# Projections' products in another order: the weights' low part last in a tile's first groups and first in its last ones

## Chip, cores and metric

The kernel runs on one core of one Trainium2 chip. The metric is the device time of one execution in microseconds. Engines: TensorE (PE; its weight loads are listed as PEld), VectorE (DVE), ScalarE (ACT), GpSimd (POOL), SyncE (SP, which issues most DMAs).

## What is computed

Two layers of a hybrid diffusion backbone over 256 latent tokens and 256 context tokens, width 1024, batch 1. Cut to what matters:

```python
for l in range(DEPTH):                       # 2 layers
    u  = modulate(layer_norm(h),  sh1, sc1)  # latent tokens
    uc = modulate(layer_norm(hc), csh1, csc1)  # context tokens
    m, mc = mixer(u, uc, w_in[l], ..., w_out[l])
    h = layer_norm_affine(DEEPNORM_ALPHA * h + g1 * m, ...)
    ...
    y = moe(tok, w_router, b_router, w_expert_gate[l], w_expert_up[l], w_expert_down[l])
    h = layer_norm_affine(DEEPNORM_ALPHA * h + g2 * y, ...)
```

Each mixer begins with a projection `u @ w_in` of all 512 tokens (1024 to 3328 columns in layer 0, to 2592 in layer 1) and ends with one, `concat(...) @ w_out` (1024 to 1024). Layer 0's mixer is windowed attention beside a two-way gated scan; layer 1's is a gated linear attention beside a Fourier mix. Behind each mixer stands a layer of 16 experts, of which each token takes two.

## The kernel before, in words

Tokens stand in four blocks of 128: 0 and 1 are context, 2 and 3 latent. Projections are made from parts: each float32 operand is split into a high part (a rounded copy, type `fp32r`, made by an ACT cast, L360 in `split`) and a low part (what the copy left out, made by a DVE subtraction, L362). `mm3` (L374 to L379) sums three of the four products of parts, high x high, high x low and low x high, for each of the 8 slices k of 128 rows: 24 products in one group, into one region of PSUM, k by k with the three interleaved. Index 0 in `PASSES` is a high part, 1 a low part.

Weights come in tiles: `load_w` reads a tile of 128 x 8 x 256 from memory into one of `NW = 3` slots `w`, on SP's queue; `split_w` (L366) makes `wh` (2 buffers) and `wl` (1 buffer) from it. In mixer 1 `cols_w` (L1123) does the same in two halves, also with two `wh` and one `wl`.

- Mixer 0 (`feat` at L704, `toks` at L710): `feat` takes the weights as the first (stationary) operand and gives features by tokens, `toks` takes them as the second (moving) operand and gives tokens by features. A tile of 256 columns has two calls (t = 0, 1), which is two groups of 24 (`feat`, 512 tokens wide) or four (`toks`, two blocks of 256 columns in each call): 96 products. The loop at L819 goes over ten tiles; the last eight are `toks`. Evictions are ACT's or DVE's (`ev_f`, `ev_hi`, `ev_gate`; `qT` at L774 with the rotary step `rope`, L719, behind it).
- Output projections (`out_proj`, L428): four weight tiles `wo` in four buffers each for high and low; a block's two halves of the output take two groups of 24 each.
- Mixer 1: three gate tiles (two groups each, blocks 2 and 3), two q tiles (two groups of 96 rows), then four tiles of keys, values and rank columns (`kvr_w`, L1241, four groups, blocks 0 to 3, 296 columns), and one for the Fourier input (`z_cols`, L1265). While gates and q run, `block` (L1143) steps blocks 0 and 1 through normalisation (`yk`, L1157), transposes by PE (L1164), modulation (ACT L1170 and DVE L1172 into `xT`) and the split into the two parts of `uT`, which the keys and values of these blocks need.

The program writes instructions in Python's order, and a scheduler of the framework then lists them on each engine by its own estimates of what is ready, within data dependencies and buffers. An engine runs its list in order, so an instruction that waits holds up all behind it. Products of a group need not stand together in PE's list.

Of the kernel before, what the change touches and what calls it, by code (L numbers as in the profile page):

```python
# [116 lines left out]
def hybrid_dit_kernel(ctx: ExitStack, tc: tile.TileContext, *aps, dbg=None, stop=99):  # L117
    nc = tc.nc
# [23 lines left out]
    def mmt():  # L142
        return mm.tile([128, 512], FP, name="mm", tag="mm")
# [222 lines left out]
    def split_w(pool, src, k, n, lobufs=1, eng=None):  # L366
        w = load_w(src, k, n)
        wh = pool.tile([128, k, n], FR, name="wh", tag="wh")
        wl = pool.tile([128, k, n], FR, name="wl", tag="wl", bufs=lobufs)
        split(wh, wl, w, eng)  # L370
        return wh, wl

    PASSES = ((0, 0), (0, 1), (1, 0))

    def mm3(ps, lhs, rhs, nk):

        for k in range(nk):
            for n, (i, j) in enumerate(PASSES):
                nc.tensor.matmul(ps, lhs(i, k), rhs(j, k), start=(k == 0 and n == 0), stop=(k == nk - 1 and n == 2))  # L379

    def xn_transpose(xT, xn, b):

# [45 lines left out]
    def out_proj(h, b, mixk, wos, g1, p):  # L428

        for n in range(2):  # L430
            ps = mmt()
            for q in range(2):
                mm3(ps[:, q * 256:(q + 1) * 256], mixk, lambda i, k: wos[n * 2 + q][i][:, k, :], 8)
            tm = p.tile([128, 512], FP, name="opt", tag="opt", bufs=2)
            cs = slice(n * 512, n * 512 + 512)
            nc.vector.tensor_tensor(tm, ps, g1[:, cs], op=OP.mult)
            nc.vector.scalar_tensor_tensor(h[b][:, cs], h[b][:, cs], ALPHA, tm, op0=OP.mult, op1=OP.add)
# [203 lines left out]
    def mixer0(s0, sr):  # L641
# [10 lines left out]
        qT = mC.tile([128, 4, 512], FP, name="qT")  # L652
# [4 lines left out]
        hqT, hi = hx[:, 0:4], hx[:, 4:8]  # L657
# [15 lines left out]
        with ExitStack() as sa:  # L673
            m1 = pool(sa, "m1")
            up = [m1.tile([128, 8, 512], FR, name=f"uT{i}") for i in range(2)]
# [17 lines left out]
            wt = split_w(m2, win[:, 512:768], 8, 256)  # L693
# [7 lines left out]
                return None  # L701
            row_bcast(snk, attn_sink[0:1, :])

            def feat(wt, o, dst_fn):  # L704

                ps = mmt()
                mm3(ps, lambda i, k: wt[i][:, k, o:o + 128], lambda i, k: up[i][:, k, :], 8)
                dst_fn(ps)

            def toks(wt, n, o, dst_fn, bp):  # L710

                ps = mmt()
                for i2 in range(2):
                    b = bp * 2 + i2
                    mm3(ps[:, i2 * n:(i2 + 1) * n], lambda i, k: up[i][:, k, b * 128:(b + 1) * 128],
                        lambda i, k: wt[i][:, k, o:o + n], 8)
                dst_fn(ps[:, 0:2 * n].rearrange("p (b n) -> p b n", b=2), bp)

            def rope(t):  # L719
                ps = trt()  # L720
                nc.tensor.matmul(ps[:, 0:256], C("perm"), t, start=True, stop=True)
                r = mq.tile([128, 256], FP, name="rot", tag="rot")
                nc.vector.tensor_tensor(r, ps[:, 0:256], C("sin"), op=OP.mult)
                nc.vector.tensor_tensor(t, t, C("cos"), op=OP.mult)
                nc.vector.tensor_tensor(t, t, r, op=OP.add)
# [45 lines left out]
            for j in range(2):  # L771
                wt = split_w(m2, win[:, j * 256:(j + 1) * 256], 8, 256)
                for t in range(2):
                    feat(wt, t * 128, lambda ps: nc.scalar.mul(qT[:, 2 * j + t, :], ps, 0.125))  # L774
                    rope(qT[:, 2 * j + t, 256:512])
            nc.vector.tensor_copy(mk[:, 0, :], C("band0"))
            nc.vector.tensor_copy(mk[:, 1, :], C("band1"))
# [41 lines left out]
            for off, ev in ((1792, None), (768, lambda i: ev_f(0, i)), (1280, lambda i: ev_f(1, i)), (2304, ev_hi),  # L819
                            (2816, ev_gate)):  # L820
                for i in range(2):
                    wt = split_w(m2, win[:, off + i * 256:off + (i + 1) * 256], 8, 256)
                    for t in range(2):
                        if ev:
                            toks(wt, 256, 0, ev(i), t)
                        else:
                            feat(wt, t * 128, lambda ps: nc.scalar.copy(hqT[:, 2 * i + t, :], ps))
                            for g_ in lws:
                                next(g_, None)

# [209 lines left out]
        wos = []  # L1040
        src = w_out_even[0]
        for n in range(4):
            w = wp.tile([128, 8, 256], FP, name="w", tag="w")
# [63 lines left out]
    def mixer1(s0, sr, h, rh, hc, y_d, pw, g2s, pre, yks, ring):  # L1107
# [6 lines left out]
        qT = m0.tile([96, 4, 256], FP, name="qT1")  # L1114

        kvr = m0.tile([128, 4, 1184], FP, name="kvr")
# [3 lines left out]
        up = [m0.tile([128, 8, 512], FR, name=f"uT1{i}") for i in range(2)]  # L1120
        mw = pool(sm, "nw", 2)

        def cols_w(o, n, ws=None):  # L1123

            wh = mw.tile([128, 8, 296], FR, name="wh", tag="wh")[:, :, 0:n]
            wl = mw.tile([128, 8, 296], FR, name="wl", tag="wl", bufs=1)[:, :, 0:n]
            for q in range(2):
                w = ws[q] if ws else load_w(win[q * 512:(q + 1) * 512, o:o + n], 4, n)
                split(wh[:, q * 4:q * 4 + 4, :], wl[:, q * 4:q * 4 + 4, :], w)
            return wh, wl  # L1130

        def toks(wt, n, b, dst_fn):

            ps = mmt()
            mm3(ps[:, 0:n], lambda i, k: up[i][:, k, b * 128:(b + 1) * 128], lambda i, k: wt[i][:, k, :], 8)
            dst_fn(ps[:, 0:n], b)

        with ExitStack() as sa:
# [52 lines left out]
            start = len(nc.cur_bb.bb.instructions)  # L1191
# [4 lines left out]
            wt = cols_w(1568, 256, pre)  # L1196
# [7 lines left out]
            for oo in (0, 256, 512):  # L1204
                wt = cols_w(1568 + oo, 256) if oo else wt
                for b in (2, 3):
                    def ev(ps, b, oo=oo):
                        o = gate[:, b - 2, oo:oo + 256]
                        nc.scalar.activation(o, ps, AF.Silu)
                        nc.vector.tensor_tensor(o, o, gnb[:, oo:oo + 256], op=OP.mult)  # L1210
                    toks(wt, 256, b, ev)
                    next(ctx_, None)
            for j in range(2):
                wt = cols_w(j * 192, 192)
                for i in range(2):
                    ps = mmt()
                    mm3(ps[0:96, 0:256], lambda p, k: wt[p][:, k, i * 96:(i + 1) * 96],
                        lambda p, k: up[p][:, k, 256:512], 8)
                    nc.scalar.mul(qT[:, 2 * j + i, :], ps[0:96, 0:256], float(96 ** -0.5))
                    next(ctx_, None)  # L1220
            for _ in ctx_:
# [19 lines left out]
        def kvr_w(i):  # L1241
            o = 296 * i
            wt = cols_w(384 + o, 296)
            for b in range(4):
                toks(wt, 296, b, lambda ps, b: (nc.scalar.copy if b % 2 else nc.vector.tensor_copy)(
                    kvr[:, b, o:o + 296], ps))
                yield

        def decays():
# [166 lines left out]
        wos = []  # L1416
        for n in range(4):
            w = load_w(w_out_odd[0][:, n * 256:(n + 1) * 256], 8, 256)
# [601 lines left out]
```

## Time and profile before

| | |
|---|---|
| median of 3 runs | 1478.98 us (1477.32 to 1482.2) |
| the profiled execution | 1483.32 us |
| its span, first to last instruction | 1481.1 us |
| mean granted TensorE clock | 0.923 |
| instructions | 18934 |

The profile is one execution; its span is what the views below divide. Times in them are microseconds from the span's start, unless a column says ns. "Granted clock" is the share of full speed that the throttle allowed the matmul engine in a stretch. A wait is idle time of an engine, put down to the instruction that ended it; `L379` is a line of the kernel, `mm<-wl,uT` the output and the inputs by the program's names.

### The profile page before, as it was taken

To read this page: it belongs to the slowest core of one execution; us is meant where nothing else is said; L and a number is where in the kernel's file an instruction comes from. 1 tells how busy PE (TensorE), PEld (TensorE's weight loads), DVE (VectorE), ACT (ScalarE), POOL (GpSimd) and SP (SyncE) were. 2 spreads that over 40 slices of the span, in tenths; PEclk is the share of its full clock that TensorE was granted. 3 is DMA by queue.
4 is the path that set the end of the run, shared out by engine and by line. 5 is a ranking of instruction groups with operands and counts; after the bars stand their busy time and mean duration, and the time that the engine had idled before them with its cause. 6 is when DMAs were issued, how large, how long until landed. Compare 5 with 4: busy or idle time off the path is not lost. (4 is left out here: it accounts for less than half of the span.)

```text
span 1481.1 us, 18934 instructions
## 1 busy us (share of the span) xinstructions
PE 1239.4 (84%) x7293; PEld 746.9 (50%) x7293; DVE 609.0 (41%) x1412; ACT 352.3 (24%) x690; POOL 94.8 (6%) x126
## 2 busy tenths in 40 slices
PE   5798888999879569999999964899977788988882
PEld 2678886445559523333333324888537443534330
DVE  4432313665657911211212169636557322223223
ACT  1422212544334111111101033442222210101001
POOL 1000001100111110110100010000010000000000
PEclk9899999999959779999999986999998799999997
DMA  8422123644011599999968953322283799988631
GB/s 274 161 87 86 62 82 99 215 159 127 2 29 72 203 357 368 372 374 340 360 243 317 355 192 101 116 64 90 86 295 127 298 393 395 387 325 312 256 144 59
DMA packets 153255, 310.30 MB, mean 210 GB/s; under 512 B 8629, under 2 KB 40693, under 8 KB 153121
## 3 DMA queue, kind: packets, MB, share of 16 engines
q1 hardware_dynamic: 145456, 293.29, 55.4%
q0 software_dynamic: 6496, 11.74, 2.2%
q10 hardware_dynamic: 1168, 3.49, 0.7%
q8 instruction: 84, 1.38, 0.4%
q14 instruction: 51, 0.41, 0.1%
HBM read 305.86 MB, written 12.06 MB: 215 GB/s over the span
## 5 line engine op out<-in xcount | busy, mean ns | idle before, releaser
L379 PE MATMUL mm<-wh,uT 128*128 128x256 f32 (+2 forms) x960 | 192.6, 297 | 4.1 <-ACT wh L360 3.7
L379 PEld LDWEIGHTS mm<-wh,uT 128*128 128x128 f32 x960 | 159.8, 200 | 10.6 <-ACT wh L360 4.4
L379 PE MATMUL mm<-wl,uT 128*128 128x256 f32 (+2 forms) x480 | 142.6, 298 | 17.0 <-DVE wl L362 17.0
L1511 PE MATMUL mm<-wx,xT 128*64 128x512 f32 x504 | 143.5, 603 | 2.8 <-ACTq L1643 1.2
L379 PEld LDWEIGHTS mm<-wl,uT 128*128 128x128 f32 x480 | 95.7, 199 | 19.9 <-DVE wl L362 19.3
L1511 PEld LDWEIGHTS mm<-wx,xT 128*64 128x64 f32 x504 | 44.9, 138 | 68.7 <-issue 66.4
L362 DVE TENSOR_TENSOR wl<-w,wh 128x2048 fp32r<-128x2048 f32 (+3 forms) x33 | 53.7, 1649 | 60.4 <-PE mm L379 59.8
L1496 DVE TENSOR_TENSOR hs<-hs,mm 64x512 f32<-64x512 f32 x32 | 22.1, 691 | 129.6 <-ACT hs L1495 83.4
L379 PE MATMUL mm<-uT,wh 128*128 128x512 f32 (+1 forms) x208 | 59.3, 374 | 6.1 <-ACT wh L360 6.1
L1511 PE MATMUL ac<-wx,xT 128*64 128x512 f32 x216 | 60.4, 595 | 3.7 <-PEq L1925 2.1
L259 PE MATMUL mm<-w,sT 128*32 128x512 f32 x296 | 52.5, 636 | 11.3 <-DVE rs L307 10.1
L379 PE MATMUL mm<-wo,mx 128*128 128x256 f32 x384 | 51.6, 293 | 6.0 <-ACT wo L360 3.5
L1518 PE MATMUL mm<-wx,hT 128*64 128x512 f32 x192 | 54.9, 597 | 1.7 <-PEq L1658 1.0
L1511 PE MATMUL tr<-wx,xT 128*64 128x512 f32 x200 | 51.8, 617 | 5.1 <-PEq L1925 2.1
L1495 ACT ACTIVATE hs<-mm 64x512 f32<-64x512 f32 x32 | 18.9, 589 | 153.7 <-PE mm L1511 103.2
L360 ACT CAST wh<-w 128x2048 fp32r<-128x2048 f32 (+3 forms) x33 | 45.7, 1387 | 34.4 <-DMA w<-in_w_in_odd_dram 16.6
L379 PEld LDWEIGHTS mm<-wo,mx 128*128 128x128 f32 x384 | 48.7, 198 | 6.8 <-ACT wo L360 3.8
L1511 PE MATMUL ac<-w,xT 128*64 128x512 f32 x104 | 44.6, 617 | 1.5 <-PEq L1925 0.8
L379 PEld LDWEIGHTS mm<-uT,wh 128*128 128x128 f32 (+1 forms) x208 | 36.9, 187 | 13.2 <-ACT wh L360 7.0
L1511 PE MATMUL mm<-w,xT 128*64 128x512 f32 x120 | 43.1, 595 | 0.5 <-PEq L1643 0.5
L1597 DVE COPY ys<-mm 64x512 f32<-64x512 f32 x22 | 15.3, 693 | 67.6 <-ACT ys L1597 64.4
L379 PE MATMUL mm<-uT,wl 128*128 128x512 f32 (+1 forms) x104 | 38.3, 375 | 3.4 <-DVE wl L362 3.4
(486 smaller groups left out, 2113.6 us busy)
## 6 DMA issues: line engine op xcount, KB each, us to landing
wx<-in_w_expert_up_dram SPq DMA_DIRECT2D x45, 1024.0 KB, 9.5
wx<-in_w_expert_gate_dram SPq DMA_DIRECT2D x42, 1024.0 KB, 7.9
wx<-in_w_expert_down_dram SPq DMA_DIRECT2D x42, 1024.0 KB, 8.5
w<-in_w_ada_dram SPq DMA_DIRECT2D x37, 1024.0 KB, 6.2
w<-in_w_expert_down_dram SPq DMA_DIRECT2D x15, 1024.0 KB, 8.7
w<-in_w_in_even_dram SPq DMA_DIRECT2D x13, 1024.0 KB, 5.1
w<-in_w_expert_gate_dram SPq DMA_DIRECT2D x12, 1024.0 KB, 9.7
w<-in_w_expert_up_dram SPq DMA_DIRECT2D x12, 1024.0 KB, 8.0
```

What stands on the lines that cost most here:

```text
L259: nc.tensor.matmul(ps[32 * g:32 * g + 32, :], sT[:, k, :], ws[k // 4][:, k % 4, :], start=k < 4, stop=k >= 4, skip_group_check=True, tile_ ...
L360: nc.scalar.copy(hi, src)
L362: nc.vector.tensor_tensor(lo, src, hi.bitcast(FP), op=OP.subtract)
L379: nc.tensor.matmul(ps, lhs(i, k), rhs(j, k), start=(k == 0 and n == 0), stop=(k == nk - 1 and n == 2))
L1495: nc.scalar.activation(hs, hp[0:64, :], AF.Silu)
L1496: nc.vector.tensor_tensor(hs, hs, hp[64:128, :], op=OP.mult)
L1511: nc.tensor.matmul(hp[i * 64:i * 64 + 64, :], xT(k), ws[2 * i + k // 4][:, k % 4, :], start=k == 0, stop=k == 7, skip_group_check=True, ti ...
L1518: nc.tensor.matmul(yp[n * 64:n * 64 + 64, :], hT[:, k, :], ws[4 + k // 2][:, k % 2, n * 512:(n + 1) * 512], start=k == 0, stop=k == 3, ski ...
L1597: (nc.vector.tensor_copy if n else nc.scalar.copy)(ys[:, ns], yp[rs_, :])
```

## The change

`mm3` no longer interleaves. It makes two lists, the eight products with the weights' low part and the sixteen others, and runs one after the other: the low ones last by default, first with `early`. The argument `w` says which operand is the weights. `early` is set for the later groups of a weight tile: the second call of a tile in mixer 0, blocks 2 and 3 of a `kvr` tile, block 3 of a gate tile, the second q group. The output projections and `z_cols` always have the low ones last. The number of products, their sizes and operands stay.

```diff
@@ -372,11 +372,14 @@
 
     PASSES = ((0, 0), (0, 1), (1, 0))
 
-    def mm3(ps, lhs, rhs, nk):
-
-        for k in range(nk):
-            for n, (i, j) in enumerate(PASSES):
-                nc.tensor.matmul(ps, lhs(i, k), rhs(j, k), start=(k == 0 and n == 0), stop=(k == nk - 1 and n == 2))
+    def mm3(ps, lhs, rhs, nk, w, early=False):
+
+
+        low = [(k, p) for p in PASSES if p[w] for k in range(nk)]
+        high = [(k, p) for k in range(nk) for p in PASSES if not p[w]]
+        order = low + high if early else high + low
+        for n, (k, (i, j)) in enumerate(order):
+            nc.tensor.matmul(ps, lhs(i, k), rhs(j, k), start=n == 0, stop=n == len(order) - 1)
 
     def xn_transpose(xT, xn, b):
 
@@ -430,7 +433,7 @@
         for n in range(2):
             ps = mmt()
             for q in range(2):
-                mm3(ps[:, q * 256:(q + 1) * 256], mixk, lambda i, k: wos[n * 2 + q][i][:, k, :], 8)
+                mm3(ps[:, q * 256:(q + 1) * 256], mixk, lambda i, k: wos[n * 2 + q][i][:, k, :], 8, 1)
             tm = p.tile([128, 512], FP, name="opt", tag="opt", bufs=2)
             cs = slice(n * 512, n * 512 + 512)
             nc.vector.tensor_tensor(tm, ps, g1[:, cs], op=OP.mult)
@@ -701,10 +704,10 @@
                 return None
             row_bcast(snk, attn_sink[0:1, :])
 
-            def feat(wt, o, dst_fn):
+            def feat(wt, o, dst_fn, early=False):
 
                 ps = mmt()
-                mm3(ps, lambda i, k: wt[i][:, k, o:o + 128], lambda i, k: up[i][:, k, :], 8)
+                mm3(ps, lambda i, k: wt[i][:, k, o:o + 128], lambda i, k: up[i][:, k, :], 8, 0, early)
                 dst_fn(ps)
 
             def toks(wt, n, o, dst_fn, bp):
@@ -713,7 +716,7 @@
                 for i2 in range(2):
                     b = bp * 2 + i2
                     mm3(ps[:, i2 * n:(i2 + 1) * n], lambda i, k: up[i][:, k, b * 128:(b + 1) * 128],
-                        lambda i, k: wt[i][:, k, o:o + n], 8)
+                        lambda i, k: wt[i][:, k, o:o + n], 8, 1, bp > 0)
                 dst_fn(ps[:, 0:2 * n].rearrange("p (b n) -> p b n", b=2), bp)
 
             def rope(t):
@@ -771,7 +774,7 @@
             for j in range(2):
                 wt = split_w(m2, win[:, j * 256:(j + 1) * 256], 8, 256)
                 for t in range(2):
-                    feat(wt, t * 128, lambda ps: nc.scalar.mul(qT[:, 2 * j + t, :], ps, 0.125))
+                    feat(wt, t * 128, lambda ps: nc.scalar.mul(qT[:, 2 * j + t, :], ps, 0.125), t > 0)
                     rope(qT[:, 2 * j + t, 256:512])
             nc.vector.tensor_copy(mk[:, 0, :], C("band0"))
             nc.vector.tensor_copy(mk[:, 1, :], C("band1"))
@@ -824,7 +827,7 @@
                         if ev:
                             toks(wt, 256, 0, ev(i), t)
                         else:
-                            feat(wt, t * 128, lambda ps: nc.scalar.copy(hqT[:, 2 * i + t, :], ps))
+                            feat(wt, t * 128, lambda ps: nc.scalar.copy(hqT[:, 2 * i + t, :], ps), t > 0)
                             for g_ in lws:
                                 next(g_, None)
 
@@ -1129,10 +1132,11 @@
                 split(wh[:, q * 4:q * 4 + 4, :], wl[:, q * 4:q * 4 + 4, :], w)
             return wh, wl
 
-        def toks(wt, n, b, dst_fn):
+        def toks(wt, n, b, dst_fn, early=False):
 
             ps = mmt()
-            mm3(ps[:, 0:n], lambda i, k: up[i][:, k, b * 128:(b + 1) * 128], lambda i, k: wt[i][:, k, :], 8)
+            mm3(ps[:, 0:n], lambda i, k: up[i][:, k, b * 128:(b + 1) * 128], lambda i, k: wt[i][:, k, :], 8, 1,
+                early)
             dst_fn(ps[:, 0:n], b)
 
         with ExitStack() as sa:
@@ -1208,14 +1212,14 @@
                         o = gate[:, b - 2, oo:oo + 256]
                         nc.scalar.activation(o, ps, AF.Silu)
                         nc.vector.tensor_tensor(o, o, gnb[:, oo:oo + 256], op=OP.mult)
-                    toks(wt, 256, b, ev)
+                    toks(wt, 256, b, ev, b > 2)
                     next(ctx_, None)
             for j in range(2):
                 wt = cols_w(j * 192, 192)
                 for i in range(2):
                     ps = mmt()
                     mm3(ps[0:96, 0:256], lambda p, k: wt[p][:, k, i * 96:(i + 1) * 96],
-                        lambda p, k: up[p][:, k, 256:512], 8)
+                        lambda p, k: up[p][:, k, 256:512], 8, 0, i > 0)
                     nc.scalar.mul(qT[:, 2 * j + i, :], ps[0:96, 0:256], float(96 ** -0.5))
                     next(ctx_, None)
             for _ in ctx_:
@@ -1243,7 +1247,7 @@
             wt = cols_w(384 + o, 296)
             for b in range(4):
                 toks(wt, 296, b, lambda ps, b: (nc.scalar.copy if b % 2 else nc.vector.tensor_copy)(
-                    kvr[:, b, o:o + 296], ps))
+                    kvr[:, b, o:o + 296], ps), b > 1)
                 yield
 
         def decays():
```

The scheduler then gives other lists. Three places follow; names end in a number for each buffer, as the program numbers them.

PE in mixer 0, where one `toks` tile (`wh_962`, `wl_963`, group `mm_1019`) ends and the next (`wh_1074`, `wl_1075`, groups `mm_1078`, `mm_1131`) begins. `uT0` and `uT1` are the high and low part of the tokens. Before:

```order
L379 MATMUL mm_1019<-wh_962,uT0_138 128x256
L379 MATMUL mm_1019<-wl_963,uT0_138 128x256
L379 MATMUL mm_1019<-wh_962,uT1_139 128x256
L379 MATMUL mm_1078<-wh_1074,uT0_138 128x256
L379 MATMUL mm_1131<-wh_1074,uT0_138 128x256
L379 MATMUL mm_1078<-wl_1075,uT0_138 128x256
L379 MATMUL mm_1078<-wh_1074,uT1_139 128x256
```

Now:

```order
L382 MATMUL mm_1019<-wh_962,uT1_139 128x256
L382 MATMUL mm_1019<-wl_963,uT0_138 128x256 x8
L382 MATMUL mm_1019<-wh_962,uT0_138 128x256
...
L382 MATMUL mm_1019<-wh_962,uT1_139 128x256
L382 MATMUL mm_1078<-wh_1074,uT0_138 128x256
L382 MATMUL mm_1078<-wh_1074,uT1_139 128x256
...
L382 MATMUL mm_1078<-wl_1075,uT0_138 128x256 x8
L382 MATMUL mm_1078<-wh_1074,uT0_138 128x256
```

Before, the old tile's last use of `wl_963` stood one product ahead of the next tile, and `wl_1075` was the third product of it. Now the eight uses of `wl_963` stand 16 products ahead of the next tile's start, and `wl_1075` comes behind 16 products on `wh_1074`.

ACT in mixer 1, between the last gate and the second tile of keys and values (`qT1` is q, `yk` and `xT1` belong to context block 1, `wh_11214` is the first `kvr` tile and `wh_11328` the second). Before:

```order
L360 CAST wh_11137<-w_11139 128x4x192
L1157 ACTIVATE yk_10875<-hc_3480,nb_11051,rs_11034 128x1024
L1219 ACTIVATE qT1_10608<-mm_11064 96x256
L360 CAST wh_11137<-w_11143 128x4x192
L360 CAST wh_11214<-w_11216 128x1184
L1219 ACTIVATE qT1_10608<-mm_11102 96x256
L1170 ACTIVATE xT1_11092<-tr_11128,cols_101 128x128 x4
L360 CAST uT10_10612<-xT1_11092 128x8x128
L1219 ACTIVATE qT1_10608<-mm_11147 96x256
L360 CAST wh_11214<-w_11220 128x1184
L1219 ACTIVATE qT1_10608<-mm_11175 96x256
L1223 ACT_TABLE_LOAD
```

Now:

```order
L360 CAST wh_11214<-w_11220 128x1184
L1223 ACTIVATE qT1_10608<-mm_11147 96x256
L1223 ACTIVATE qT1_10608<-mm_11175 96x256
L1227 ACT_TABLE_LOAD
L360 CAST wh_11328<-w_11330 128x1184
L1161 ACTIVATE yk_10875<-hc_3480,nb_11051,rs_11034 128x1024
L360 CAST wh_11328<-w_11334 128x1184
L1174 ACTIVATE xT1_11092<-tr_11128,cols_101 128x128 x4
L360 CAST uT10_10612<-xT1_11092 128x8x128
```

`yk` and the evictions of block 1's transposes stood among the q evictions; now they stand behind the last of them, the table load and a cast of the next tile. On DVE the two halves of the split `wl_11215` likewise moved from behind that block's steps into them, ahead of the row `nb_11051` that `yk` needs.

PE at the same place: block 1's transposes `tr_11093` and `tr_11128` and the first `kvr` tile's groups (`mm_11224` for block 0, `mm_11250` for block 1, `mm_11276` for block 2). Before:

```order
L379 MATMUL mm_11102<-uT10_10612,wh_11054 96x256
L1164 MATMUL tr_11093<-cst_86,yk_10875 128x128 x4
L379 MATMUL mm_11102<-uT11_10613,wh_11054 96x256
...
L379 MATMUL mm_11102<-uT10_10612,wl_11055 96x256
L1164 MATMUL tr_11128<-cst_86,yk_10875 128x128 x4
L379 MATMUL mm_11224<-wh_11214,uT10_10612 128x296
L379 MATMUL mm_11147<-uT10_10612,wl_11138 96x256
...
L379 MATMUL mm_11250<-wh_11214,uT10_10612 128x296
L379 MATMUL mm_11276<-wh_11214,uT10_10612 128x296
L379 MATMUL mm_11302<-wh_11214,uT10_10612 128x296
L379 MATMUL mm_11224<-wl_11215,uT10_10612 128x296
```

Now:

```order
L382 MATMUL mm_11224<-wh_11214,uT11_10613 128x296
L382 MATMUL mm_11224<-wl_11215,uT10_10612 128x296 x8
L1168 MATMUL tr_11093<-cst_86,yk_10875 128x128 x4
L1168 MATMUL tr_11128<-cst_86,yk_10875 128x128 x4
L1256 MATMUL tr_11364<-cst_86,kvr_10609 32x128
L382 MATMUL mm_11250<-wh_11214,uT10_10612 128x296
L382 MATMUL mm_11276<-wl_11215,uT10_10612 128x296 x8
L382 MATMUL mm_11276<-wh_11214,uT10_10612 128x296
L382 MATMUL mm_11250<-wh_11214,uT11_10613 128x296
```

The transposes stood among the second q group's products and ahead of most of block 0's group; now they stand behind all of block 0's group, and one product of block 1's group stands right behind them, ahead of the groups of the other blocks.

SP's and POOL's lists are the same before and after.

## Rows read from the trace of the kernel before

**Rows 1.** The page's part 1: engine, busy us, share of the span, instructions.

```profile
PE 1239.4 (84%) x7293; PEld 746.9 (50%) x7293; DVE 609.0 (41%) x1412; ACT 352.3 (24%) x690; POOL 94.8 (6%) x126
```

**Rows 2.** Table by stretches: us, busy PE, PEld, DVE, ACT, POOL, clock, DMA share, GB/s.

```profile
47.00:240.00 193.00, 170.34 (x1111) 155.76 (x1111) 56.23 (x65) 47.55 (x54) 2.08 (x3) 0.94 0.24 79
...
500.00:900.00 400.00, 335.17 (x1567) 129.03 (x1567) 115.32 (x279) 60.45 (x101) 41.84 (x45) 0.93 0.89 322
```

**Rows 3.** PE's waits, 45 to 240 us: us in total, times, longest.

```profile
PE mm L379 <- DVE wl L362: 16.6, 9, 2.3
PE mm L379 <- ACT wh L360: 6.1, 3, 3.7
PE tr L721 <- ACT qT L774: 1.9, 1, 1.9
```

**Rows 4.** Groups by line and shape, 126 to 240: busy, mean ns | idle before, releaser.

```profile
L379 PE MATMUL mm<-wl,uT 128*128 128x256 f32 x254 | 75.2, 297 | 14.6 <-DVE wl L362 14.6
...
L362 DVE TENSOR_TENSOR wl<-w,wh 128x2048 fp32r<-128x2048 f32 x7 | 16.0, 2293 | 27.8 <-PE mm L379 27.8
```

**Rows 5.** Table by stretches, one for each tile (two of seven), their sum, and one stretch.

```profile
136.81:150.62 13.81, 11.58 (x96) 11.58 (x96) 4.97 (x6) 2.98 (x3) 0.00 (x0) 1.00 0.24 77
150.62:165.91 15.29, 13.26 (x98) 13.05 (x96) 4.98 (x6) 2.98 (x4) 0.00 (x0) 0.89 0.23 70
...
sum 102.59, PE 88.03 PEld 86.61 DVE 28.63 ACT 19.17 POOL 0.00; mean PE 12.58 PEld 12.37 DVE 4.09 ACT 2.74 POOL 0.00
...
154.42:157.83 3.41, 3.41 (x19) 3.41 (x18) 0.00 (x0) 0.00 (x0) 0.00 (x0) 0.50 0.85 288
```

**Rows 6.** Timeline at a tile's end: start, us, engine, line, names [idle before <-releaser].

```profile
150.30 0.52 PE L379 MATMUL mm<-wh,uT 128*128 128x256 f32 x3
150.50 2.29 DVE L362 TENSOR_TENSOR wl<-w,wh 128x2048 fp32r<-128x2048 f32 x1 [3.47 <-PE mm L379]
...
151.11 1.89 ACT L360 CAST wh<-w 128x2048 fp32r<-128x2048 f32 x1
...
152.85 0.39 PE L379 MATMUL mm<-wl,uT 128*128 128x256 f32 x1 [2.03 <-DVE wl L362]
```

**Rows 7.** The page's part 5, products and weight loads on one pair of names.

```profile
L379 PE MATMUL mm<-wh,uT 128*128 128x256 f32 (+2 forms) x960 | 192.6, 297 | 4.1 <-ACT wh L360 3.7
L379 PEld LDWEIGHTS mm<-wh,uT 128*128 128x128 f32 x960 | 159.8, 200 | 10.6 <-ACT wh L360 4.4
```

**Rows 8.** Timeline of PE in output projection 0.

```profile
450.30 3.02 PE L379 MATMUL mm<-wo,mx 128*128 128x256 f32 x23 [0.77 <-DVE wo L362]
```

**Rows 9.** PE's waits, 900 to 966 us.

```profile
PE mm L379 <- ACT wh L360: 3.7, 4, 1.4
PE mm L379 <- DVE wl L362: 3.2, 4, 1.3
```

**Rows 10.** Timeline of ACT in mixer 1, and of PE behind the first `kvr` tile.

```profile
940.26 1.24 ACT L1157 ACTIVATE yk<-hc,nb,rs 128x1024 f32<-128x1024 f32 x1 [5.00 <-DVE nb L1156]
...
944.83 1.48 ACT L1170 ACTIVATE xT<-tr,cols 128x128 f32<-128x128 f32 x4
946.34 1.05 ACT L360 CAST uT<-xT 128x1024 fp32r<-128x1024 f32 x1
...
950.33 0.38 ACT L1219 ACTIVATE qT<-mm 96x256 f32<-96x256 f32 x1 [0.47 <-PE mm L379]
950.72 1.28 ACT L1223 ACT_TABLE_LOAD   x1
952.01 1.19 ACT L360 CAST wh<-w 128x1184 fp32r<-128x1184 f32 x1
...
964.66 0.81 PE L1252 MATMUL tr<-cst,kvr 128*32 128x128 f32 x4
```

**Rows 11.** Timeline of ACT and PE in output projection 1.

```profile
1108.93 1.90 ACT L360 CAST wo<-w 128x2048 fp32r<-128x2048 f32 x1 [6.58 <-DMA w<-in_w_out_odd_dram]
...
1113.20 7.63 PE L379 MATMUL mm<-wo,mix 128*128 128x256 f32 x48 [1.75 <-DVE wo L362]
```

## The prediction

> **What bounds the kernel now.** The engine totals come first: the matmul engine (PE) is busy 84% of the span [rows 1], so what can be won is its idle time and the time it runs at half clock. The table by stretches comes next. In the first mixer's projections, 47 to 240 us, PE is busy 170 of 193 us at a granted clock of 0.94, while DVE (56 us), ACT (48 us) and the DMA engines (0.24) have room; in the first expert stage, 500 to 900 us, the DMA engines are 0.89 busy and the reads of weights set the pace [rows 2]. The table of waits then tells what PE waits for in the projections: 16.6 us in nine waits for `wl`, the low part of the weights, 6.1 us for `wh`, 1.9 us for an eviction [rows 3]. The groups by line put 14.6 of the 16.6 into the seven tiles after 126 us, and show on DVE the other half of the same loop: the split that writes `wl` takes 2.29 us and DVE was idle 27.8 us before it, waiting for PE's last product with the old `wl` [rows 4]. There is one buffer for `wl`, and before the change a tile's last group uses it to its last product but one and the next tile's first group wants it at its second. The table by tiles shows the same as a period: seven tiles take 102.59 us, and one that met no half clock has 11.58 us of work in 13.81 us [rows 5]. The timeline shows one turn of it: PE's last products of a tile start at 150.30, the split runs from 150.50 to 152.79, PE goes on at 152.85, 2.03 us idle; the `wh` cast behind it, at 151.11, is already the one for the tile after [rows 6].
>
> **The change part by part.**
>
> *Products.* The same 24 per group, in the same number. A tile's 96 products at full clock take 11.58 us, 0.121 each [rows 5], and I take that price for the new order too; the rival below is the case in which it is wrong.
>
> *Mixer 0, the seven tiles.* By the order, a tile's last `wl` product is now followed by 16 high ones of its second group and 16 high ones of the next tile's first group, all on `wh`, which was cast a tile ahead. 32 x 0.121 = 3.9 us of cover against 2.29 us of split plus some 0.1 to 0.2 us of hand-over at each end [rows 4, 6]. So the wait goes to nothing, with 1.2 us to spare. What is late next: the split is also behind whatever DVE does at that time, which is one 0.7 us eviction at most; the `wh` cast (1.89 us) has a whole tile. The seven tiles should take 7 x 11.58 = 81.1 us instead of 102.6 [rows 5]: 21.5 us less. Of that 14.6 are waits. The rest is mainly half clock: a tile with such a stretch takes 15.29 instead of 13.81 us, 1.5 us more, and there are four such tiles, 5.9 us; the stretch lies right behind the gap (154.42 to 157.83 at 0.50, which is 1.2 GHz; 1.00 is 2.4) [rows 5]. I let these go with the gaps.
>
> *Mixer 0, before 126 us.* The other `wl` waits are 16.6 - 14.6 = 2.0 us and go in the same way. Of the `wh` waits the longest, 3.7 us, is the start of the stage and stays; 6.1 - 3.7 = 2.4 go, since they came from the scheduler's putting first products of later groups ahead, on weights not yet cast, and the new order no longer does. The 1.9 us wait of the rotary product for `qT` [rows 3] was an eviction queued behind a cast of the 1.89 us kind [rows 6]; in ACT's new order the eviction stands first, which leaves some 0.3: 1.6 us. With 21.5 that makes 27.5; I take 27, for hand-overs that now show. Ends: 27.5, and 18.6 (waits alone: 14.6 + 2.0 + 2.0) if every half clock stays.
>
> *Output projection 0.* Low last, no early groups. PE stops at 450.30 for the low part of a later tile [rows 8]; the order has 24 products of the first two groups left behind that point instead of 33, so 9 x 0.121 = 1.1 us. Ends: 0, if DVE's split is what comes late, and 1.1.
>
> *Mixer 1's first part.* What can go are the waits for `wh` and `wl`, 3.7 + 3.2 = 6.9 us [rows 9]. But here the scheduler also moves the chain of context block 1 (normalise, transpose, modulate, split) behind other work. On ACT the normalised row `yk` (1.24 us) now stands behind both last q evictions (0.38), a table load (1.28) and a cast (1.19) [rows 10]; with 0.2 of hand-over that is 4.3 us after PE's last q product, and PE has one group of 24 products of 296 columns meanwhile, 24 x 0.121 x 296/256 = 3.4 us. So PE waits about 1.0 us before the transposes. Then one product of the next group (block 1) heads PE's queue, and with it all products of blocks 2 and 3 behind it wait for ACT's four evictions (1.48) and the cast of `uT` (1.05) [rows 10], with 0.4 of hand-overs 2.9 us. 6.9 - 1.0 - 2.9 = 3.0 us less. Ends: 6.9 less, if the chain comes in time, and 3 more (second rival).
>
> *Output projection 1.* Its second tile lands late: the cast at 1108.93 waits 6.58 us for the DMA, and nothing saved before counts against that. Behind it PE waits 1.75 us for the low part [rows 11]. Now 16 products on the cast alone, 1.9 us, run while the split (2.29, with hand-overs 2.45) is made: 0.55 us of wait is left, 1.2 us less. Ends: 0 and 1.75.
>
> *Other stages.* SP's and POOL's order does not change. The expert stages, bound by DMA [rows 2], begin when the mixer and the router before them end, and shift along. Nothing for them.
>
> Sum: 27 + 1.1 + 3 + 1.2 = 32.3 us against the profiled execution's 1483.3: 1451.0. The median of the runs stands 4.3 us below that execution, so 1446.7; I say **1447**.
>
> **The rivals.**
>
> *The half clock stays.* For it: PE's work per tile stays dense, and the rows show stretches at half clock elsewhere without telling what set them off; also a tile with the same kind of gap ran at 1.00 [rows 5], so the gap alone did not decide. Then 4 x 1.5 = 6 us are not won: 1453. Against it: each stretch in the tiles lies right behind a gap. The Trainium skill, "TensorE: Matmul & The Clock Gate", section "Why this matters for your kernels", lets the clock fall only behind idle gaps longer than these 2 us; by it these four stretches would have another cause and stay, which is this rival. The trace speaks against it here: 0.89 in tiles whose only idle time is that gap [rows 5]. Chance 0.13.
>
> *Block 1's chain eats mixer 1's gain.* `uT` of block 1 was ready at 947.4 on ACT [rows 10]. By the order, ahead of `yk` there are now on ACT a table load and one cast more, 2.5 us, and on DVE, in the middle of the reciprocal root, a split of 2 x 1184 columns, 2.29 x 2368/2048 = 2.65 us; with the two casts of kvr's first weights, 2.4 us, the chain could end 7.5 us later, at 955. PE has then three groups left, 3 x 3.4 = 10.2, and ends at 965.2 against 964.66 now [rows 10], and 1 to 2.5 us more with half clock behind the wait: up to 3 us lost instead of 3 won, 1453; with the first rival's loss in it too, 1459. It decides where `yk` comes over 4 us after the last q product. Against it: DVE has the chain's first part done early, and its own waits were for PE. Chance 0.16.
>
> *The split is not covered.* If DVE takes the split 1.2 us late in each tile, waits come back; at the worst the tiles keep all and 1483.3 - 32.3 + 21.5 = 1472.5 is left, 1468 on the median, and about 1474 with mixer 1's gain lost as well. Against it: DVE is busy 56 of 193 us. Chance 0.05.
>
> *Slower: the array pays for reloading.* Products with low weights as the moving operand used to follow one with the same stationary operand. In the projections to tokens (480) and the output projections (192) the new order parts these 672 pairs. If the second of a pair had its load for nothing, each would now show a load of 200 ns [rows 7] against a product of 121 ns, 79 ns more, 53 us: 1447 + 53 = 1500. It decides at 32.3/672 = 48 ns a pair. Against it: every product has a load of its own already, 960 loads for 960 products [rows 7], and the spacing is 0.121 us over whole tiles in which parted and unparted neighbours alternate. Chance 0.02. The Trainium skill, same page, section "Step-by-step: what each phase is for", says that a loaded operand can serve many products; rows 7 show that this program doesn't use it.
>
> *The change does nothing.* Excluded: the order shows the moved rows.
>
> **How the numbers follow.** Forecast 0.62, the rivals 0.13, 0.16, 0.05 and 0.02; 0.02 for an unforeseen event that leaves no difference. Low end: 1447 less what the other ends give (mixer 1: 3.9, output 1: 0.55, mixer 0: 0.5) and some 5 us, chosen, for half clock outside these parts that may go too (0.93 in the expert stage [rows 2]): 1437. High end: both first rivals together, 1459, and output projections at nothing, 1461; 1462. That leaves out the last two rivals and the unforeseen. A measurement of this kernel tells 0.3%, 4.4 us, from no change: faster has the forecast, the first two rivals and most of the third, 0.95; same 0.03; slower 0.02.
>
> **What would show it.** Right: between 137 and the end of the projections no wait for `wl` over 0.3 us, tiles of 11.6 us, clock 1.00 there; DVE's wait for PE in front of each split still long; the projections' end some 27 us earlier, at about 212. In mixer 1 a new wait of the block-1 transposes for `yk`, about 1 us, and one of a product for `uT`, about 3. Wrong: tiles at 11.6 but spacing over 0.121 us (reloading); 0.89 in tiles without gaps (first rival); a wait for `uT` of over 6 us (second); splits that start over 1 us after PE's last low product (third).

## The result, and the profile after

The changed kernel takes 1445.95 us, median of four runs (1442.95 to 1449.03), beside 1480.59 for the kernel before: a ratio of 0.9764, 95% interval 0.9735 to 0.9793. Run again with the experiments below, it took 1441.46 beside 1479.28, 0.9743 (0.9719 to 0.9767). The forecast was 1447, in a range of 1437 to 1462. The profiled execution took 1449.03 us, its span 1446.7, 34.4 under the span before.

The engine totals [rows 1] hardly move: the same 7293 products, 3 us less busy time, in a span 34 us shorter. The time came out of what PE did not do.

```profile
PE 1236.1 (85%) x7293; PEld 739.6 (51%) x7293; DVE 607.7 (42%) x1412; ACT 353.5 (24%) x690; POOL 93.6 (6%) x126
```

The table by stretches of the changed kernel (columns as in [rows 2]): mixer 0's projections from the first product to the last, one `toks` tile, and the last seven tiles together.

```profile
47.92:208.52 160.60, 160.31 (x1111) 149.06 (x1111) 55.82 (x64) 46.31 (x52) 1.51 (x2) 0.98 0.28 91
127.72:139.24 11.52, 11.52 (x99) 11.52 (x98) 5.07 (x6) 2.99 (x3) 0.00 (x0) 1.00 0.30 92
...
127.72:208.52 80.80, 80.80 (x674) 80.59 (x672) 27.48 (x26) 19.20 (x19) 0.00 (x0) 1.00 0.29 92
```

The tile has no idle time left, 11.52 of 11.52 us; against [rows 5], seven tiles take 80.8 us instead of 102.6, at full clock. (The count of 99 takes in products that overlap the edge of the stretch.)

PE's waits from 45 to 215 us, to hold against [rows 3]:

```profile
PE mm L382 <- ACT wh L360: 3.7, 1, 3.7
PE mm L927 <- ACT f L360: 2.0, 1, 2.0
PE tr L948 <- POOL kk L920: 0.7, 1, 0.7
PE tr L724 <- ACT qT L760: 0.3, 1, 0.3
```

No wait for `wl` is left; the 3.7 us at the start stays; the `qT` wait behind a cast is gone. The two lines in the middle belong to the recurrence, which now starts inside this stretch. The timeline at a tile's end, and the split on DVE by line, answer to [rows 6] and [rows 4]:

```profile
137.52 2.29 DVE L362 TENSOR_TENSOR wl<-w,wh 128x2048 fp32r<-128x2048 f32 x1 [1.79 <-PE mm L382]
138.28 3.04 PE L382 MATMUL mm<-wh,uT 128*128 128x256 f32 x24
...
141.16 1.12 PE L382 MATMUL mm<-wl,uT 128*128 128x256 f32 x8
```

```profile
L362 DVE TENSOR_TENSOR wl<-w,wh 128x2048 fp32r<-128x2048 f32 x7 | 16.0, 2292 | 16.0 <-PE mm L382 16.0
```

The split takes the same 2.29 us and DVE still waits for PE in front of it, but it is done at 139.81, and PE comes to the first low product at 141.16: 1.35 us to spare, where 1.2 was forecast.

In mixer 1, PE's waits from 870 to 940 us and its timeline there (before: [rows 9, 10]):

```profile
PE tr L1168 <- ACT yk L1161: 21.2, 2, 20.3
PE mm L382 <- ACT uT L360: 2.2, 1, 2.2
PE tr L1256 <- DVE xT L1176: 1.0, 1, 1.0
```

```profile
914.72 1.09 PE L1168 MATMUL tr<-cst,yk 128*128 128x128 f32 x8 [0.85 <-ACT yk L1161]
916.84 0.40 PE L1256 MATMUL tr<-cst,kvr 128*32 128x128 f32 x1 [1.02 <-DVE xT L1176]
919.40 0.62 PE L382 MATMUL mm<-wh,uT 128*128 128x296 f32 x1 [2.17 <-ACT uT L360]
```

The 20.3 us stand in both kernels, ahead of the first product. The waits of 3.7 and 3.2 us for `wh` and `wl` are gone, and the forecast's new ones are there: 0.85 us for `yk`, then 1.02 + 2.17 = 3.2 us until `uT` of block 1 is written.

The timeline of PE in output projection 0, which answers to [rows 8], and in output projection 1, which answers to [rows 11]:

```profile
420.51 2.78 PE L382 MATMUL mm<-wo,mx 128*128 128x256 f32 x21 [1.58 <-DVE wo L362]
```

```profile
1077.11 10.38 PE L382 MATMUL mm<-wo,mix 128*128 128x256 f32 x72 [6.70 <-ACT wo L360]
```

In the first, PE now stops for the same late split 0.8 us longer, with fewer products left behind it; in the second the wait for the cast stays and the 1.75 us behind it is gone.

By stage, from first product to last, before and now: mixer 0's projections 191.7 and 160.6 us; output projection 0 60.3 and 59.7; mixer 1's projections 128.1 and 125.0; output projection 1 38.6 and 36.8. Between the stages nothing moves by more than about 1 us; the last stage, from the end of output projection 1 to the end, is 1.6 us longer in this execution.

### The profile page after: what moved, and what is told of

Same layout as the page of the kernel before. It is cut to its first block, busy times and chain, and to the rows that moved or that the text cites. A ratio compares the mean times of both kernels' runs of the same rounds, so it can differ in the third digit from the quotient of the medians.

```text
span 1446.7 us, 18929 instructions
## 1 busy us (share of the span) xinstructions
PE 1236.1 (85%) x7293; PEld 739.6 (51%) x7293; DVE 607.7 (42%) x1412; ACT 353.5 (24%) x690; POOL 93.6 (6%) x126
## 5 line engine op out<-in xcount | busy, mean ns | idle before, releaser
L382 PE MATMUL mm<-wh,uT 128*128 128x256 f32 (+2 forms) x960 | 131.5, 292 | 2.5 <-ACT uT L360 2.2
L382 PEld LDWEIGHTS mm<-wh,uT 128*128 128x128 f32 x960 | 124.9, 194 | 5.6 <-ACT uT L360 2.5
L382 PE MATMUL mm<-wl,uT 128*128 128x256 f32 (+2 forms) x480 | 69.7, 292 | 0.1
L382 PEld LDWEIGHTS mm<-wl,uT 128*128 128x128 f32 x480 | 63.9, 194 | 3.3 <-issue 2.4
L1515 PE MATMUL ac<-wx,xT 128*64 128x512 f32 x216 | 60.3, 595 | 3.7 <-PEq L1929 2.1
L382 PE MATMUL mm<-uT,wh 128*128 128x512 f32 (+1 forms) x208 | 45.7, 374 | 3.7 <-ACT wh L360 3.7
L382 PEld LDWEIGHTS mm<-uT,wh 128*128 128x128 f32 (+1 forms) x208 | 36.3, 189 | 10.1 <-ACT wh L360 3.8
L1515 PE MATMUL mm<-wm,xT 128*64 128x512 f32 x80 | 36.2, 597 | 0.3 <-PEq L1647 0.2
```

The costliest lines, as they stand in the source:

```text
L382: nc.tensor.matmul(ps, lhs(i, k), rhs(j, k), start=n == 0, stop=n == len(order) - 1)
L1515: nc.tensor.matmul(hp[i * 64:i * 64 + 64, :], xT(k), ws[2 * i + k // 4][:, k % 4, :], start=k == 0, stop=k == 7, skip_group_check=True, ti ...
```

## The experiments

The theory: the time lay in the turn of mixer 0's one `wl` buffer, and the new order covers the split with products that don't need it. Rivals: the moved pairs of products, the early groups, mixer 1's share, and a half clock that has its own cause.

**The change in mixer 0 alone**

```diff
-                mm3(ps[:, q * 256:(q + 1) * 256], mixk, lambda i, k: wos[n * 2 + q][i][:, k, :], 8, 1)
+                mm3_i(ps[:, q * 256:(q + 1) * 256], mixk, lambda i, k: wos[n * 2 + q][i][:, k, :], 8, 1)
...
-            mm3(ps[:, 0:n], lambda i, k: up[i][:, k, b * 128:(b + 1) * 128], lambda i, k: wt[i][:, k, :], 8, 1,
+            mm3_i(ps[:, 0:n], lambda i, k: up[i][:, k, b * 128:(b + 1) * 128], lambda i, k: wt[i][:, k, :], 8, 1,
...
-                    mm3(ps[0:96, 0:256], lambda p, k: wt[p][:, k, i * 96:(i + 1) * 96],
+                    mm3_i(ps[0:96, 0:256], lambda p, k: wt[p][:, k, i * 96:(i + 1) * 96],
```

`mm3_i` is the interleaving function of before. Expected:

> The change in mixer 0 alone; output projections and mixer 1 interleave as before. Theory (the turn of the one `wl` buffer in mixer 0 carries the gain): mixer 0's projections, first product to last, take about 161 us as in the changed kernel (192 before), mixer 1's and the output projections' stretches are as before, and the time lies about 31 us under before, 1448 to 1451, 3 to 5 us over the changed kernel. Rival (the later parts carry a good share): 1455 to 1460.

Measured: 1451.53 us, just above the 1448 to 1451 expected, ratio 0.9821 (0.9781 to 0.9862). Mixer 0's projections 160.5 us, mixer 1's 129.0, output projections 60.1 and 39.3: each stage as the theory has it. Against the changed kernel's two medians the rest of the change is worth 5.6 us (1445.95) or 10.1 (1441.46), against 27 that mixer 0 alone brings (1478.82, the kernel before beside it): mixer 0 carries most, though the rest is more than the 3 to 5 us expected.

**Low part last everywhere, never first**

```diff
-        order = low + high if early else high + low
+        order = high + low
```

> Low part last in every group, never first. A tile's last product then uses `wl`, and the cover of the split is only what stands in front of the next tile's first low product: by the order 16 products of its first group and 5 of its second, 21 x 0.121 = 2.5 us against 2.45 us of split and hand-overs. Theory (cover against split decides): waits of 0 to 0.3 us a tile, mixer 0's projections 161 to 164 us, no half clock in the tiles, time within 4 us of the changed kernel in mixer 0; in mixer 1 the gain may be another. Rival (the early groups are what matters): waits near 2 us a tile remain, mixer 0's projections 175 us or more.

Measured: 1448.11 us, 0.9793 (0.9757 to 0.9829); mixer 0's projections 161.5 us. One tile, and the timeline where it begins:

```profile
150.80:162.45 11.65, 11.65 (x98) 11.58 (x97) 4.97 (x5) 3.00 (x4) 0.00 (x0) 1.00 0.29 91
```

```profile
150.80 2.68 PE L382 MATMUL mm<-wh,uT 128*128 128x256 f32 x21
151.01 2.29 DVE L362 TENSOR_TENSOR wl<-w,wh 128x2048 fp32r<-128x2048 f32 x1 [3.11 <-PE mm L382]
...
153.35 1.22 PE L382 MATMUL mm<-wl,uT 128*128 128x256 f32 x8
```

The split ends at 153.30, the first low product starts at 153.35. The 21 products in front of it nearly hold it: 11.65 us a tile instead of 11.52, 0.13 us of delay. So the early groups add little in mixer 0: the 16 + 5 products of the next tile are almost cover enough, and `early` makes them 32. The rival falls.

**The old order with three half buffers**

```diff
-        wl = pool.tile([128, k, n], FR, name="wl", tag="wl", bufs=lobufs)
-        split(wh, wl, w, eng)
-        return wh, wl
+        nc.scalar.copy(wh, w)
+        wl = [pool.tile([128, 4, n], FR, name="wl", tag="wl", bufs=3) for _ in range(2)]
+        for q in range(2):
+            s = slice(q * 4, q * 4 + 4)
+            nc.vector.tensor_tensor(wl[q], w[:, s, :], wh[:, s, :].bitcast(FP), op=OP.subtract)
+        return wh, Halves(wl)
```

`Halves` picks the half of a slice k. The products' order within a group is that of before, in every stage.

> The order of products as before, but mixer 0's low part in three buffers of half a tile (4 of 8 slices each) instead of one of a whole tile, split in two steps. Theory (one buffer's turn is the cause): the next tile's first half can be split while the last tile still runs, so the waits for `wl` at the tile changes (14.6 us before) and the half clock behind them (5.9 us) go without any new order: mixer 0's projections about 165 to 172 us instead of 192, waits of `wh` and `qT` kept. Rival (the order of the products is what matters): 185 us or more.

Measured: 1451.38 us, 0.9804 (0.9769 to 0.9839); mixer 0's projections 160.6 us, as in the changed kernel. A tile, and the half splits on DVE:

```profile
139.45:150.97 11.52, 11.52 (x98) 11.52 (x97) 5.22 (x6) 2.99 (x3) 0.00 (x0) 1.00 0.28 92
```

```profile
L381 DVE TENSOR_TENSOR wl<-w,wh 128x1024 fp32r<-128x1024 f32 x14 | 17.2, 1225 | 28.7 <-PE mm L390 18.4 <-ACT wh L377 10.2
```

This run decides most. With the program's order of before, the buffer alone takes away all that the change takes away in mixer 0, and more than I expected: the waits for `wh` and for `qT` go too (only the 3.7 us at the start and 0.3 for a `qT` stay). So they hang on the `wl` wait and are no faults of their own. My reading, which no run tests by itself: the scheduler, seeing a wait for `wl` ahead, put first products of later groups in front, and these ran into weights not yet cast. The run also settles the reloading: here the `toks` products with the same stationary operand stand next to each other, in the changed kernel they don't, and both have tiles of 11.52 us. The parted pairs cost nothing that can be seen.

**The split on POOL**

```diff
-                    wt = split_w(m2, win[:, off + i * 256:off + (i + 1) * 256], 8, 256)
+                    wt = split_w(m2, win[:, off + i * 256:off + (i + 1) * 256], 8, 256, 1, nc.gpsimd)
```

> The changed kernel with the subtraction that makes `wl` in mixer 0's ten tiles of the loop on POOL in place of DVE. The one such subtraction that POOL has in the kernel before took 4.88 us, so the cover of 32 products, 32 x 0.12 = 3.84 us, no longer holds it. Theory (cover against split decides): a wait of 4.88 + 0.2 - 3.84 = 1.2 us at each change of tiles from `toks` to `toks`, seven or eight of them, 8 to 10 us; mixer 0's projections 169 to 171 us; if a gap of this size calls the half clock too, up to 6 us more, 177. Rival (the projections no longer hang on the split at all, the new order has cured it by something else): 161 us.

Measured: 1460.72 us, 0.9875 (0.9842 to 0.9908), 19 us over the changed kernel run beside it (1441.46, below). PE's waits in the projections, one of them in the timeline, and a tile:

```profile
PE mm L382 <- POOL wl L364: 12.8, 8, 5.4
```

```profile
136.55 1.22 PE L382 MATMUL mm<-wl,uT 128*128 128x256 f32 x8 [1.07 <-POOL wl L364]
```

```profile
133.41:146.25 12.84, 11.77 (x98) 11.57 (x97) 4.88 (x4) 2.98 (x3) 4.61 (x2) 1.00 0.26 83
```

Seven waits of 1.07 us for a split of 4.61 us, in tiles of 12.84: cover against split, where 1.2 us was forecast from a split of 4.88. None of these seven tiles ran at half clock. An eighth wait, 5.4 us, is of a `feat` tile and was not forecast; the timeline there, and the granted clock behind it:

```profile
112.98 5.45 PE L382 MATMUL mm<-uT,wl 128*128 128x512 f32 x16 [5.39 <-POOL wl L364]
```

```profile
112.84:116.25 3.41, 3.27 (x8) 2.60 (x9) 0.00 (x0) 0.00 (x0) 0.09 (x1) 0.50 0.64 185
```

POOL began the split behind this wait 7.3 us after its last other work, and the trace names nothing that held it. With it the projections took 176.5 us, not 169 to 171, and here half clock followed.

**The new order in mixer 1 alone**

```diff
-                mm3(ps[:, q * 256:(q + 1) * 256], mixk, lambda i, k: wos[n * 2 + q][i][:, k, :], 8, 1)
+                mm3_i(ps[:, q * 256:(q + 1) * 256], mixk, lambda i, k: wos[n * 2 + q][i][:, k, :], 8, 1)
...
-                mm3(ps, lambda i, k: wt[i][:, k, o:o + 128], lambda i, k: up[i][:, k, :], 8, 0, early)
+                mm3_i(ps, lambda i, k: wt[i][:, k, o:o + 128], lambda i, k: up[i][:, k, :], 8, 0, early)
...
-                    mm3(ps[:, i2 * n:(i2 + 1) * n], lambda i, k: up[i][:, k, b * 128:(b + 1) * 128],
+                    mm3_i(ps[:, i2 * n:(i2 + 1) * n], lambda i, k: up[i][:, k, b * 128:(b + 1) * 128],
```

> The new order in mixer 1 alone; mixer 0 and the output projections interleave. Theory (parts add up): mixer 0's projections 191 to 192 us with the waits for `wl` of before, mixer 1's from first to last product 125 us as in the changed kernel (128 before), with a wait for `yk` of 0.9 and of about 3 us in all for `uT`, time 1476 to 1478. Rival (mixer 1's gain comes from mixer 0's, which starts it earlier against its loads): 128 us.

Measured, one run: 1480.55 us, above the 1476 to 1478 expected; one run can't tell such a difference. Mixer 1's projections took 123.0 us, so its gain doesn't come from mixer 0's; the waits were 0.85 us for `yk`, as expected, and 1.0 and 1.4 until `uT`, shorter than the 3 expected. Mixer 0's took 188.0, not 191 to 192, with the very waits of before:

```profile
PE mm L388 <- DVE wl L362: 16.6, 9, 2.3
PE mm L388 <- ACT wh L360: 6.1, 3, 3.7
```

What differs is the clock in the tiles. Two rows of seven; the other five are like the first:

```profile
151.35:165.16 13.81, 11.78 (x99) 11.58 (x98) 4.97 (x5) 2.98 (x3) 0.00 (x0) 1.00 0.24 77
...
220.47:235.92 15.45, 13.42 (x98) 13.02 (x96) 3.59 (x3) 1.19 (x2) 0.00 (x0) 0.89 0.21 69
```

One tile of seven at half clock behind its gap, where the first profile had four. So the kernel before was profiled twice more.

**The kernel before, two more executions** (no edit)

> The kernel before once more, for how often its 2 us gaps are followed by half clock: four of the seven tiles in the first profile. Theory (the stretch depends on where the gap falls, so its number changes from one execution to the next): 0 to 4 of seven tiles, the seven tiles 97 to 103 us, waits for `wl` as in the first profile. Rival (it is fixed by the program's place): the same four tiles, 103 us.

> The same a third time: theory, again another number of tiles at half clock; rival, the same four.

Measured: 1477.96 and 1480.66 us. The tile at half clock of the first and the sum of its seven tiles, then the sum of the second's:

```profile
163.75:179.05 15.30, 13.27 (x98) 13.07 (x97) 4.97 (x5) 2.98 (x3) 0.00 (x0) 0.89 0.22 70
...
sum 98.62, PE 84.07 PEld 82.44 DVE 28.74 ACT 19.17 POOL 0.00; mean PE 12.01 PEld 11.78 DVE 4.11 ACT 2.74 POOL 0.00
```

```profile
sum 100.05, PE 85.50 PEld 83.88 DVE 28.75 ACT 19.17 POOL 0.00; mean PE 12.21 PEld 11.98 DVE 4.11 ACT 2.74 POOL 0.00
```

One tile and two tiles at half clock, with 16.6 us of waits for `wl` each time. So with the same program and the same gaps the number changes from one execution to the next: 4, 1 and 2, and 1 in the run above. The theory holds, the rival of a fixed place falls.

**Keys and values in the order of blocks 2, 3, 0, 1**

```diff
-            for b in range(4):
+            for b in (2, 3, 0, 1):
                 toks(wt, 296, b, lambda ps, b: (nc.scalar.copy if b % 2 else nc.vector.tensor_copy)(
-                    kvr[:, b, o:o + 296], ps), b > 1)
+                    kvr[:, b, o:o + 296], ps), b < 2)
```

This undoes what the change lost in mixer 1: the groups that need context block 1 go last.

> The changed kernel with the groups of keys and values taken in the order of blocks 2, 3, 0, 1, so that what needs context block 1 stands last. Theory (in mixer 1 the new order gives back some 3.5 us in waits for block 1's `yk` and `uT`, and a stretch at half clock behind them): waits for `yk` and `uT` go, mixer 1's first part is 3 to 5 us shorter than in the changed kernel, time 1441 to 1443. Rival (what follows, the decays and the scan, waits for the same chain anyway): the waits come back behind the keys and values, time as the changed kernel.

Measured: 1438.06 us, below the 1441 to 1443 expected, 0.9709 (0.9681 to 0.9738); mixer 1's projections 117.7 us, 7.3 under the changed kernel's profile. PE's timeline there:

```profile
912.41 1.09 PE L1168 MATMUL tr<-cst,yk 128*128 128x128 f32 x8
913.26 1.60 PE L382 MATMUL mm<-wh,uT 128*128 128x296 f32 x10
...
926.96 0.91 PE L1261 MATMUL mm<-hc 33*128 33x384 f32 x2 [0.33 <-DVE hc L1257]
```

No wait is left in front of the transposes or of block 1's group, and the decays start 51.0 us after the stage's first product, not 58.1. That is more than the forecast 3 to 5: the profile of the changed kernel also had 6.83 us at half clock behind these waits, which cost half of that. To compare on one chip, both were run again together.

> The changed kernel itself, beside the next one on the same chip: 1443 to 1449, ratio to before 0.976 to 0.979.

> The changed kernel with the order of blocks 2, 3, 0, 1 in the keys and values once more, beside the changed kernel on the same chip: theory, 6 to 8 us under it (its mixer 1 was 7.3 us shorter); rival (the 8 us between the two medians was the chips' difference): 0 to 3 us under it.

Measured: the changed kernel 1441.46 us, 0.9743 (0.9719 to 0.9767), a little under what was expected; with the new order of blocks 1436.94, 0.9722 (0.9697 to 0.9748): 4.5 us less, between theory and rival; the intervals overlap. The stretch from mixer 1's first product to the decays, first in the changed kernel, then with the order of blocks:

```profile
876.30:931.60 55.30, 50.85 (x383) 48.85 (x382) 42.72 (x90) 28.69 (x43) 2.58 (x7) 0.96 0.45 134
```

```profile
873.10:924.10 51.00, 50.15 (x384) 48.33 (x382) 42.55 (x90) 27.76 (x43) 2.57 (x7) 0.96 0.48 142
```

In the stretch 4.3 us less, 3.6 of it idle time of PE (4.45 against 0.85); this time the changed kernel met no half clock behind its waits. So in this pair the order of blocks is worth 4.3 us, and in the first pair, where the clock fell too, some 3 more. It is the version to take: its median is lower than the changed kernel's in both comparisons.

## Why the prediction was right

**The bound and the mechanism.** Right, and shown from three sides: the waits go when the order is changed, they go as completely when the buffer is changed and the order kept, and they come back at 1.07 us when the split is made longer than its cover.

**Mixer 0's tiles.** Forecast 21.5 us off 102.6; the profiled pair gives 102.6 to 80.8, 21.8. But one term of it was a draw: 5.9 us of half clock were in the profile that I worked from, and 1.5 to 3 in three other profiles of the same gaps. For a median the term should have been about half. The 4.3 us taken off to go from the profiled execution to the median may hold part of it a second time: the executions with one and two such tiles took 1477.96 and 1480.66 us, the one with four 1483.32. The runs don't separate the two. "I let these go with the gaps" held: in the tiles of the changed kernel (both profiles), of mixer 0 alone, of low last, of the half buffers and of the order of blocks (both profiles) there is no stretch at half clock. The low end of 18.6 is a slip: by the forecast's own waits it is 14.6 + 2.0 + 2.4 + 1.6 = 20.6. The time and the range don't use it.

**Mixer 0, the first part.** Forecast 6.0 us of waits; 89.1 us became 79.8, 9.3 less. Waits account for 6.4 (the `qT` wait and two each for `wl` and `wh`), and about 1.2 comes from the stretch at half clock at the stage's start, of which 7.8 us lay behind the first product before and 5.3 now; the rest I can't place. The step that named the scheduler's first products as a cause of their own was off: by the half-buffer run they go with the `wl` wait.

**Output projections.** Forecast 1.1 and 1.2. Six profiles with interleaved products have 60.1 to 60.3 and 38.6 to 40.2 us, six with the new order 59.4 to 59.7 and 36.2 to 38.3: about 0.7 and 2.1. Both small; the second was undersized. In the first, the nine products fewer behind the stop are there (96 done ahead of it, 87 before), but the stop is 0.8 us longer, so less than the 1.1 is left. The wait for the loads, 6.7 us, stayed as forecast.

**Mixer 1.** Forecast 3.0 net, with 6.9 taken away and 1.0 + 2.9 given back. Given back in the profile: 0.85 + 3.2; in two other profiles without half clock during these waits (the change in mixer 1 alone, and the changed kernel again) 0.85 + about 2.4. Net in the profiled pair 3.1; over more profiles, interleaved 128.1 to 130.1 us against 122.0 to 125.0, about 5, in which half clock behind the waits moves each by a few us. The rival in which block 1's chain eats the gain didn't come: what it gives back is 4.0 of 6.9 us, where the forecast had 3.9.

**The rivals.** The half clock that stays: it went. The Trainium skill, "TensorE: Matmul & The Clock Gate", section "Why this matters for your kernels", ties the fall to longer idle gaps; here it fell behind gaps of about 2 us in 8 of 28 tiles (four profiles), in none of the seven with 1.07 us, and behind the one of 5.4. The uncovered split: 1.35 us to spare. Reloading: refuted by equal tiles with and without the pairs.

**The sum.** 32.3 forecast, 34.4 in the profiled pair, 34.6 and 37.8 between medians. Stage by stage from more profiles: mixer 0 about 28.6 (189.1, mean of four with the old turn, to 160.5), output projections 0.7 and 2.1, mixer 1 about 5. The forecast's terms were 27, 2.3 and 3: mixer 1 was the most undersized. That the time came within about 1 us of 1447 is partly luck: a half clock taken some 3 us too high stood against terms sized too low, mixer 0's first part by 3.3, output projection 1 by 0.9 and mixer 1 by 2.

## To carry to other kernels

A single buffer that is written from a result and read to the end by the consumer can cost about its write time at every turn (here 2.03 to 2.27 us for a write of 2.29), whatever the engines' busy shares say; look for two idle times that name each other. It can be cured by order (use the buffer early in the last group and late in the first one) or by a buffer of half the size more. The order can be priced beforehand as products in between against the time of the write; for the buffer the expectation of 165 to 172 us was too high by 4 us and more. When a reordering lets a list scheduler move other chains, look for the first group in the queue that needs the moved chain, and put it last; in this kernel that was worth 4.3 us.

## What was not expected of the hardware

The same program with the same 2 us gaps met half clock behind 4, 1 and 2 of seven of them in three executions, each 1.5 us: how many one profile shows is a draw, and what they cost the kernel is a mean over profiles: 2 of 7 tiles and 3 us, with the run of mixer 1 alone as the fourth. Gaps of 1.07 us met none in seven. The subtraction of 128 x 2048 took 4.61 us on POOL in these tiles, where the one in the kernel before took 4.88, and 2.29 on DVE. Between products 256 columns wide, whether the next one has the same stationary operand made no difference: 11.52 us for 96 of them either way.
